# A decoder trunk on one core: layer B's softmax per token tile, attention begun with its k, and two projections moved ahead

## The chip, the cores and the metric

The kernel runs on one core of one Trainium2 chip. The metric is the time of one execution on the device in microseconds; the kernel before was timed in three runs. Beside them one execution was taken by the hardware profiler. Its page and its trace are what is read below. Engines are named PE (TensorE matmul), DVE (VectorE), ACT (ScalarE), POOL (GpSimd) and SP (SyncE, which issues the weight DMAs here).

## What is computed

A two-layer decoder trunk on 256 tokens of width 1024, all in float32. Layer A is a causal differential attention with an MLP. Then one set of keys and values is projected, and layer B attends to it: three groups of dilated windows, 16 heads of width 64, and an MLP. Cut to layer B, which the change touches:

```python
def dilated_mixer(x, norm_gain, w_q, q_gain, w_o, k_sh, v_sh, cos, sin):
    q = (rms_norm(x, norm_gain) @ w_q).reshape(B, S, G, H, D)
    q = rms_norm(q, q_gain[:, None, :])
    q = apply_rope(q.reshape(B, S, G * H, D), cos, sin).reshape(B, S, G, H, D)
    for g, (window, dilation) in enumerate(DIL_GROUPS):     # (128,1), (512,4), (2048,16)
        o_g, lse_g = dilated_group_attention(q[:, :, g], k_sh[:, :, g], v_sh[:, :, g], window, dilation)
    wts = jax.nn.softmax(jnp.stack(lses, axis=0), axis=0)   # over the three groups
    o = jnp.sum(wts[..., None] * jnp.stack(outs, axis=0), axis=0)
    return o.astype(x.dtype).reshape(B, S, H * D) @ w_o
```

Weighting the groups by their softmax denominators is the same as one softmax over the scores of all three groups, and so the kernel computes it.

## The kernel before

Every float32 product is made of three matmuls: both operands are split into a high part (ACT, a copy to the reduced type) and a low part (DVE, the difference). The weights arrive by DMA from SP in pieces of 768 KB or 1 MB (`raw`), and class `Weights` splits each half of a piece into `whi` and `wlo` (L82, L83), up to five halves ahead of their use.

Layer B works on eight pairs of heads, `hp` 0 to 7. For each pair the loop at L719 projects q (i = 0), k (i = 1) and the values (i = 2), each 384 columns for two token tiles of 128: `gemm` (L297) makes four calls of `gemm_half`, of 12 matmuls each (L292 to L294). `qk_rows` (L310) turns a tile of q or k into normalized, rotated rows: a square on ACT, the product `T` and the sums on DVE, three operations on POOL that end in `qn`. The value tiles `vt` are split on ACT and DVE (L731, L732).

The attention of a pair, `attn_B` (L596), is a Python generator. `start` puts it on a list, and `tick` (L211) lets each entry of the list go on to its next `yield`, after it has pumped the weight splits. `gemm` ticks after its first three halves and the loop at L735 once more at the end of a projection. A generator that yields n goes on n ticks later. So the numbers in `WAIT_B` say how much projection work is issued on PE between two steps of a pair's attention. The steps are:

1. `qk_T` (L352): 12 transposes of q and k rows on PE (L357), split into `th` (ACT) and `tl` (DVE).
2. Scores of tile 0 (L350) and, a step later, of tile 1. Masked passes on DVE (L369) write `sm` and the maxima.
3. The softmax: `nm` (DVE), exponentials with row sums (L618, ACT), reciprocal `rd` (DVE), scaling (L623, ACT).
4. For each of the two heads: 8 transposes of the probabilities (L632), split into `p2` (L634); then 6 matmuls with the values (L646), `ot` on ACT and DVE (L649, L650), `oT` on POOL (L651). After the second head `oT` is split into `oh` (`oTh`, ACT) and `ol` (`oTl`, DVE).

The loop over pairs before the change starts the attention of a pair after its third projection:

```python
pss = acc0 if hp == 0 and i == 0 else gemm(hx, ("B", hp, i), 384)
...
tick()
...
gens.append(start(attn_B(hp, rows[0], rows[1], vts, oh, ol)))
```

After the last projection class `OutProj` (L390) multiplies with `woB`: `body(kt)` for pairs 0 to 5, two groups of six 512-column matmuls each with a tick behind each group, and `group` (L413) for pairs 6 and 7, inside `boundary` (L372). Before these the kernel finishes the generators that are still active (L738 to L742). Pieces of weights are planned in the order of their use (L138 to L144).

The pools bound how far work can run ahead: eight PSUM banks for everything on PE, two buffers each of `sm`, `p2` and `T`, four of `th` and `tl`, three of the value tiles, six of `qn`. Within these the framework's scheduler may place an instruction on an engine earlier or later than its line in the program.

Of the kernel before, what the change touches and what calls it, by code (L numbers as in the profile page):

```python
# [10 lines left out]
F32 = mybir.dt.float32  # L11
# [5 lines left out]
P = 128  # L17
S = 256
NT = S // P
# [21 lines left out]
WAIT_B = (2, 2, 2, 2, 2, 3)  # L41

SUB = ((2, 0, 4), (3, 1, 5))

# [58 lines left out]
def trunk(ctx, tc, a):  # L103
# [17 lines left out]
    def plan(key, src, n):  # L121
        at[key] = len(chunks)
        chunks.append((src, n))
# [14 lines left out]
    for hp in range(HP):  # L138
        for i in range(3):
            for j in range(2):  # L140
                plan(("B", hp, i, j), a["wB"][hp, i, j], 4 * 384)
# [80 lines left out]
    def start(gen):  # L222
        ent = [gen, 0]
        active.append(ent)
        return ent
# [137 lines left out]
    def block(b):  # L363
        return slice(b * P, (b + 1) * P)
# [231 lines left out]
    def attn_B(hp, qr, kr, vts, oh, ol):  # L596
# [3 lines left out]
        mxs = [small.tile([P, 2], F32, name="mx", tag="mx") for _ in range(2)]  # L600
        sms = [wk.tile([P, 2, 4 * P], F32, name="sm", tag="sm") for _ in range(2)]
        for b in range(2):
            own = slice(S + b * P, S + (b + 1) * P)
            scs = [wps(), wps()]
            scores2([sc[:, 0:S] for sc in scs], T0, block(b), KALL)
            scores2([sc[:, S:S + P] for sc in scs], T1, block(b), own)
            scores2([sc[:, S + P:] for sc in scs], T2, block(b), own)
            for hh in range(2):
                masked(sms[hh][:, b, :], scs[hh], mask[:, 4 * b:4 * b + 4, :].rearrange("p b k -> p (b k)"),
                       -3e38, mxs[hh][:, b:b + 1])  # L610
            yield WAIT_B[2 + b]
        for hh in range(2):
            sm = sms[hh]
            den = small.tile([P, 2], F32, name="den", tag="den")
            nm = small.tile([P, 2], F32, name="nm", tag="nm")
            nc.vector.tensor_scalar(nm, mxs[hh], -(HD ** -0.5), None, op0=ALU.mult)
            for b in range(2):
                nc.scalar.activation(sm[:, b, :], sm[:, b, :], AF.Exp, bias=nm[:, b:b + 1], scale=HD ** -0.5,  # L618
                                     accum_out=den[:, b:b + 1])
            rd = small.tile([P, 2], F32, name="rd", tag="rd")  # L620
            nc.vector.reciprocal(rd, den)
            for b in range(2):
                nc.scalar.activation(sm[:, b, :], sm[:, b, :], AF.Copy, scale=rd[:, b:b + 1])  # L623
        yield WAIT_B[2]
# [94 lines left out]
    for hp in range(HP):  # L719
        rows = [[None] * NT, [None] * NT]  # L720
        vts = []
        for i, hx in ((0, hq), (1, hk), (2, hk)):
            pss = acc0 if hp == 0 and i == 0 else gemm(hx, ("B", hp, i), 384)
            for t in range(NT):
                ps = pss[t]
                if i < 2:
                    rows[i][t] = qk_rows(ps, 2 * G, rb[NT + t], windows(tabB[:, i, t]))
                else:
                    vt = wk.tile([P, 2 * G, 2, HD], F32R, name="v", tag="v", bufs=3)
                    psv = ps[:, :384].rearrange("p (g d) -> p g d", d=HD)  # L730
                    nc.scalar.activation(vt[:, :, 0, :], psv, AF.Copy, scale=rb[t])  # L731
                    nc.vector.scalar_tensor_tensor(vt[:, :, 1, :], psv, rb[t], vt[:, :, 0, :].bitcast(F32),  # L732
                                                   op0=ALU.mult, op1=ALU.subtract)
                    vts.append(vt)
            tick()  # L735
        gens.append(start(attn_B(hp, rows[0], rows[1], vts, oh, ol)))
# [94 lines left out]
```

## Time and profile before

| | |
|---|---|
| Median of 3 runs | 800.8 us (800.39 to 802.36) |
| Profiled execution, its own time | 801.55 us |
| Span of the profile | 799.5 us |
| Busy: PE, weight loads (PEld), DVE, ACT, POOL | 97%, 86%, 73%, 58%, 24% |
| Mean granted TensorE clock | 0.995 of full speed |
| DMA | 131.12 MB, mean 164 GB/s |

The span runs from the first to the last instruction of the profiled execution. Layer B's projections and attention lie from about 320 to 606 us, its output projection from 577 to 616 us, the second MLP behind it. A row of the timeline gives the start and the duration of one instruction or of a run of alike ones (x8), its engine, line, operation, out<-in, shapes, and in brackets how long the engine stood idle before it and who released it. PE matmuls overlap, so their starts are what counts.

### The profile page before, as it was taken

How to read it: one execution, taken by the hardware profiler on the slowest of the kernel's cores; microseconds unless marked ns; L12 is line 12 of the kernel's file. 1: busy time of each engine (PE TensorE's matmuls, PEld its weight loads, DVE VectorE, ACT ScalarE, POOL GpSimd, SP SyncE). 2: the span in 40 equal slices, each digit the busy share in tenths (PEclk: the TensorE clock that was granted, in tenths of full speed). 3: DMA queues.
4: the chain of work that ended last, by engine and by line, in shares of the span. 5: the costliest groups of instructions: out<-in, count | busy, mean ns of one | idle time of the engine just before them, and what ended most of it. 6: DMA issues, size and time to landing. Idle time of an engine off the chain costs nothing.

```text
span 799.5 us, 11766 instructions
## 1 busy us (share of the span) xinstructions
PE 772.1 (97%) x4408; PEld 686.7 (86%) x4408; DVE 581.1 (73%) x985; ACT 467.0 (58%) x851; POOL 190.9 (24%) x191
## 2 busy tenths in 40 slices
PE   6999989999999999999999999999997999999998
PEld 6898967888888888999999999999886888888886
DVE  3998987666656666998888888888767666556663
ACT  5667777544444445657586674857766544444441
POOL 2553531300000000555336354363611000000000
PEclk9999999999999999999999999999999999999999
DMA  8643445445555542554443434434442455545531
GB/s 300 229 143 123 158 155 164 169 171 197 198 176 207 171 184 90 187 198 154 136 153 113 157 121 157 158 119 172 159 158 106 158 186 182 210 170 199 187 130 52
DMA packets 22328, 131.12 MB, mean 164 GB/s; under 512 B 2560, under 2 KB 3328, under 8 KB 13056
## 3 DMA queue, kind: packets, MB, share of 16 engines
q1 hardware_dynamic: 22272, 130.38, 46.0%
q8 instruction: 34, 0.56, 0.3%
q14 instruction: 22, 0.18, 0.1%
HBM read 129.32 MB, written 1.05 MB: 163 GB/s over the span
## 4 chain that ended last, share of the span: by engine, by line
PE 64%; DVE 17%; ACT 12%; issue 3%; POOL 2%; DMA 1%; SPq 0%; POOLq 0%; DVEq 0%; ACTq 0%
PE wps L435 15%; PE wps L437 7%; PE acc L488 7%; PE acc L489 7%; PE acc L490 7%; DVE wlo L83 5%; PE acc L292 4%; PE acc L294 4%; PE acc L293 4%; ACT whi L82 4%; ACT sm L618 2%; DVE sm L369 2%; PE wps L632 2%; DVE T L317 2%; ACT smA L541 2%
## 5 line engine op out<-in xcount | busy, mean ns | idle before, releaser
L83 DVE TENSOR_TENSOR wlo<-raw,whi 128x1024 fp32r<-128x1024 f32 (+1 forms) x272 | 307.0, 1138 | 153.9 <-ACT whi L82 153.7
L82 ACT ACTIVATE whi<-raw 128x1024 fp32r<-128x1024 f32 (+1 forms) x272 | 258.9, 957 | 211.1 <-issue 74.9
L435 PE MATMUL wps<-hT,whi 128*128 128x512 f32 x512 | 182.2, 399 | 2.0 <-DVE hT L271 2.0
L437 PE MATMUL wps<-hT,wlo 128*128 128x256 f32 x512 | 142.9, 280 | 0.0
L435 PEld LDWEIGHTS wps<-hT,whi 128*128 128x128 f32 x512 | 95.9, 188 | 26.0 <-DVE hT L271 3.2
L328 POOL TENSOR_TENSOR T<-T 128x384 f32<-128x384 f32 (+1 forms) x48 | 44.4, 924 | 280.5 <-DVE ms L243 181.6
L488 PE MATMUL acc<-whi,u 128*128 128x512 f32 x256 | 100.4, 392 | 0.3 <-ACT u L340 0.3
L489 PE MATMUL acc<-wlo,u 128*128 128x512 f32 x256 | 100.0, 391 | 0.0
L490 PE MATMUL acc<-whi,u 128*128 128x512 f32 x256 | 98.9, 389 | 0.0
L437 PEld LDWEIGHTS wps<-hT,wlo 128*128 128x128 f32 x512 | 96.6, 189 | 1.4
L292 PE MATMUL acc<-whi,hT 128*128 128x384 f32 x256 | 88.8, 349 | 0.3 <-ACT whi L82 0.2
L292 PE MATMUL acc<-whi,hK 128*128 128x384 f32 x256 | 87.6, 343 | 0.0
L293 PE MATMUL acc<-wlo,hT 128*128 128x384 f32 x256 | 86.3, 337 | 1.1 <-DVE wlo L83 1.1
L294 PE MATMUL acc<-whi,hT 128*128 128x384 f32 x256 | 86.2, 337 | 0.0
L294 PE MATMUL acc<-whi,hK 128*128 128x384 f32 x256 | 85.8, 335 | 0.0
L293 PE MATMUL acc<-wlo,hK 128*128 128x384 f32 x256 | 85.7, 335 | 0.0
L332 POOL TENSOR_TENSOR f<-ms,half 128x6 f32<-128x6 f32 (+1 forms) x48 | 68.2, 1422 | 4.6 <-DVE ms L323 3.1
L488 PEld LDWEIGHTS acc<-whi,u 128*128 128x128 f32 x256 | 48.1, 188 | 11.7 <-ACT u L340 1.2
L490 PEld LDWEIGHTS acc<-whi,u 128*128 128x128 f32 x256 | 48.1, 188 | 10.6 <-DVE u L341 0.4
L489 PEld LDWEIGHTS acc<-wlo,u 128*128 128x128 f32 x256 | 48.1, 188 | 8.8
L293 PEld LDWEIGHTS acc<-wlo,hT 128*128 128x128 f32 x256 | 48.6, 190 | 1.4 <-DVE wlo L83 1.4
L292 PEld LDWEIGHTS acc<-whi,hT 128*128 128x128 f32 x256 | 48.6, 190 | 1.4 <-ACT whi L82 0.5
(117 smaller groups left out, 1204.9 us busy)
## 6 DMA issues: line engine op xcount, KB each, us to landing
raw<-in_wB SPq DMA_DIRECT2D x48, 768.0 KB, 4.2
raw<-in_wup SPq DMA_DIRECT2D x32, 1024.0 KB, 4.8
raw<-in_wdn SPq DMA_DIRECT2D x32, 1024.0 KB, 4.8
raw<-in_wA SPq DMA_DIRECT2D x15, 768.0 KB, 4.3
raw<-in_woA SPq DMA_DIRECT2D x4, 1024.0 KB, 4.8
raw<-in_woB SPq DMA_DIRECT2D x4, 1024.0 KB, 4.8
early<-in_x SPq DMA_DIRECT2D x2, 512.0 KB, 5.3
x<-in_xp SPq DMA_DIRECT2D x1, 1024.0 KB, 7.5
```

Of the source, the lines that this page charges most:

```text
L82: self.nc.scalar.activation(hi[:, :n], raw, AF.Copy)
L83: self.nc.vector.tensor_tensor(lo[:, :n], raw, hi[:, :n].bitcast(F32), op=ALU.subtract)
L292: nc.tensor.matmul(ps, h[:, kt, 0, tok], wh[:, c], start=kt == 0, stop=False)
L293: nc.tensor.matmul(ps, h[:, kt, 0, tok], wl[:, c], start=False, stop=False)
L294: nc.tensor.matmul(ps, h[:, kt, 1, tok], wh[:, c], start=False, stop=kt == KT - 1)
L328: nc.gpsimd.tensor_tensor(u[:, :n].rearrange("p (h a d) -> p h a d", a=2, d=HD // 2), T[:, 0, :n].rearrange("p (h a d) -> p h a d", a=2, d ...
L332: nc.gpsimd.tensor_tensor(f[:, :nsub], ms[:, :nsub], half[:, :nsub], op=ALU.pow)
L435: nc.tensor.matmul(o, wh[:, c], self.h[:, kt].rearrange("p l s -> p (l s)"), start=kt == 0, stop=False, skip_group_check=True)
L437: nc.tensor.matmul(o[:, 0:S], wl[:, c], self.h[:, kt, 0, :], start=False, stop=kt == KT - 1, skip_group_check=True)
L488: nc.tensor.matmul(ps, uh[:, tok], dh[:, c], start=first, stop=False)
L489: nc.tensor.matmul(ps, uh[:, tok], dl[:, c], start=False, stop=False)
L490: nc.tensor.matmul(ps, ul[:, tok], dh[:, c], start=False, stop=last)
```

## The change

Three things are done together.

- `attn_B` does the softmax of both heads for tile 0 right behind the scores of tile 0, and that of tile 1 behind the scores of tile 1. `mx`, `nm`, `den` and `rd` hold two heads of a tile where they held two tiles of a head.
- A pair's attention is started after its k projection instead of after its values; `WAIT_B` is changed with it.
- A list `PAIRS` gives the order of projections. It is the old one for pairs 0 to 5; then come q and k of pair 6, q and k of pair 7, the values of pair 6, the values of pair 7. The weight pieces are planned in that order.

```diff
-WAIT_B = (2, 2, 2, 2, 2, 3)
+WAIT_B = (4, 2, 2, 3, 2, 3)
...
+PAIRS = [(hp, i) for hp in range(HP - 2) for i in range(3)]
+PAIRS += [(HP - 2 + e, i) for e, i in ((0, 0), (0, 1), (1, 0), (1, 1), (0, 2), (1, 2))]
...
-    for hp in range(HP):
-        for i in range(3):
-            for j in range(2):
-                plan(("B", hp, i, j), a["wB"][hp, i, j], 4 * 384)
+    for hp, i in PAIRS:
+        for j in range(2):
+            plan(("B", hp, i, j), a["wB"][hp, i, j], 4 * 384)
...
-        mxs = [small.tile([P, 2], F32, name="mx", tag="mx") for _ in range(2)]
         sms = [wk.tile([P, 2, 4 * P], F32, name="sm", tag="sm") for _ in range(2)]
         for b in range(2):
...
+            mx = small.tile([P, 2], F32, name="mx", tag="mx")
             for hh in range(2):
                 masked(sms[hh][:, b, :], scs[hh], mask[:, 4 * b:4 * b + 4, :].rearrange("p b k -> p (b k)"),
-                       -3e38, mxs[hh][:, b:b + 1])
-            yield WAIT_B[2 + b]
-        for hh in range(2):
-            sm = sms[hh]
+                       -3e38, mx[:, hh:hh + 1])
+            nm = small.tile([P, 2], F32, name="nm", tag="nm")
+            nc.vector.tensor_scalar(nm, mx, -(HD ** -0.5), None, op0=ALU.mult)
             den = small.tile([P, 2], F32, name="den", tag="den")
-            nm = small.tile([P, 2], F32, name="nm", tag="nm")
-            nc.vector.tensor_scalar(nm, mxs[hh], -(HD ** -0.5), None, op0=ALU.mult)
-            for b in range(2):
-                nc.scalar.activation(sm[:, b, :], sm[:, b, :], AF.Exp, bias=nm[:, b:b + 1], scale=HD ** -0.5,
-                                     accum_out=den[:, b:b + 1])
+            for hh in range(2):
+                nc.scalar.activation(sms[hh][:, b, :], sms[hh][:, b, :], AF.Exp, bias=nm[:, hh:hh + 1],
+                                     scale=HD ** -0.5, accum_out=den[:, hh:hh + 1])
             rd = small.tile([P, 2], F32, name="rd", tag="rd")
             nc.vector.reciprocal(rd, den)
-            for b in range(2):
-                nc.scalar.activation(sm[:, b, :], sm[:, b, :], AF.Copy, scale=rd[:, b:b + 1])
-        yield WAIT_B[2]
+            for hh in range(2):
+                nc.scalar.activation(sms[hh][:, b, :], sms[hh][:, b, :], AF.Copy, scale=rd[:, hh:hh + 1])
+            yield WAIT_B[2 + b]
...
-    for hp in range(HP):
-        rows = [[None] * NT, [None] * NT]
-        vts = []
-        for i, hx in ((0, hq), (1, hk), (2, hk)):
-            pss = acc0 if hp == 0 and i == 0 else gemm(hx, ("B", hp, i), 384)
...
-            tick()
-        gens.append(start(attn_B(hp, rows[0], rows[1], vts, oh, ol)))
+    rows, vts = {}, [[] for _ in range(HP)]
+    for hp, i in PAIRS:
+        hx = hk if i else hq
+        pss = acc0 if hp == 0 and i == 0 else gemm(hx, ("B", hp, i), 384)
...
+        tick()
+        if i == 1:
+            gens.append(start(attn_B(hp, *[[rows[hp, e, t] for t in range(NT)] for e in range(2)], vts[hp],
+                                     oh, ol)))
```

## Rows read from the trace of the kernel before

**Rows 1.** Busy time by stretch, pair 3: length, PE, PEld, DVE, ACT, POOL, clock, DMA.

```profile
439.20:473.00 33.80, 33.24 (x223) 31.68 (x222) 27.82 (x48) 22.67 (x41) 15.78 (x16) 1.00 0.42 141
```

**Rows 2.** Timeline of PE, pair 0: start us, us, engine, line, operation.

```profile
370.26 0.33 PE L294 MATMUL acc<-whi,hK 128*128 128x384 f32 x1
...
370.78 0.34 PE L294 MATMUL acc<-whi,hK 128*128 128x384 f32 x1
...
371.75 0.42 PE L292 MATMUL acc<-whi,hK 128*128 128x384 f32 x1
```

**Rows 3.** Waits of PE, 345 to 575 and 575 to 622: total us, times, longest.

```profile
PE wps L632 <- ACT sm L623: 3.9, 6, 1.0
...
PE wps L646 <- DVE p L341: 0.9, 1, 0.9
```

**Rows 4.** Timeline of PE around the transposes of pair 2's probabilities.

```profile
437.28 0.34 PE L294 MATMUL acc<-whi,hK 128*128 128x384 f32 x1
438.20 1.27 PE L632 MATMUL wps<-ident,sm 128*128 128x128 f32 x8 [0.58 <-ACT sm L623]
439.23 0.42 PE L292 MATMUL acc<-whi,hK 128*128 128x384 f32 x1
```

**Rows 5.** Timeline of PE at the end of the output projection's bodies.

```profile
605.58 0.40 PE L404 MATMUL acc<-whi,oTl 128*128 128x512 f32 x1
606.92 1.22 PE L646 MATMUL wps<-p,v 128*128 128x512 f32 x6 [0.94 <-DVE p L341]
610.78 0.53 PE L402 MATMUL acc<-whi,oTh 128*128 128x512 f32 x1 [2.65 <-ACT oTh L340]
...
614.53 1.04 PE L260 MATMUL wps<-ident,x 128*128 128x128 f32 x8
```

**Rows 6.** Timeline of PE, pair 3, from pair 2's last PV on.

```profile
452.96 1.10 PE L646 MATMUL wps<-p,v 128*128 128x512 f32 x6
453.89 0.33 PE L292 MATMUL acc<-whi,hK 128*128 128x384 f32 x1
...
456.10 0.39 PE L350 MATMUL wps<-th,tl 64*128 64x256 f32 x2
...
462.84 0.44 PE L292 MATMUL acc<-whi,hK 128*128 128x384 f32 x1
...
471.99 1.27 PE L632 MATMUL wps<-ident,sm 128*128 128x128 f32 x8 [0.56 <-ACT sm L623]
```

**Rows 7.** Busy time by stretch, behind the long wait of the tail.

```profile
610.70:614.50 3.80, 3.72 (x9) 2.80 (x10) 1.81 (x3) 1.04 (x4) 0.00 (x0) 0.55 0.51 216
```

**Rows 8.** Timeline of ACT, the scaling passes of pair 2.

```profile
437.44 2.54 ACT L623 ACTIVATE sm<-sm,rd 128x512 f32<-128x512 f32 x4
```

**Rows 9.** Timeline of DVE and ACT, the softmax of pair 7.

```profile
593.47 0.68 DVE L369 CUSTOM_DVE_ANT_0 sm<-wps,mask 128x512 f32<-128x512 f32 x1
...
595.61 0.71 ACT L618 ACTIVATE sm<-sm,nm 128x512 f32<-128x512 f32 x1
...
597.02 1.32 ACT L623 ACTIVATE sm<-sm,rd 128x512 f32<-128x512 f32 x2
...
598.96 1.04 ACT L82 ACTIVATE whi<-raw 128x1024 fp32r<-128x1024 f32 x1
```

**Rows 10.** Timeline of DVE, rows of q, and the end of pair 2's attention.

```profile
453.31 0.94 DVE L317 TENSOR_TENSOR T<-acc,tabB 128x768 f32<-128x768 f32 x1
...
457.18 0.68 DVE L650 TENSOR_TENSOR ot<-wps,ot 64x512 f32<-64x512 f32 x1
...
460.97 0.42 DVE L341 TENSOR_TENSOR oTl<-oT,oTh 128x256 fp32r<-128x256 f32 x1 [1.98 <-ACT oTh L340]
```

**Rows 11.** Waits of all engines, 340 to 620: total us, times, longest.

```profile
ACT oTh L340 <- POOL oT L651: 24.7, 8, 3.5
```

**Rows 12.** Timeline of POOL and PE in pair 0's k rows and pair 1's q.

```profile
346.00 0.83 POOL L334 TENSOR_TENSOR qn<-T,f 128x384 f32<-128x384 f32 x1
...
346.03 0.33 PE L292 MATMUL acc<-whi,hT 128*128 128x384 f32 x1
```

More of the change, by code (lines that the diff above doesn't have):

```diff
@@ L718, in trunk @@
     gens = []
-    for hp in range(HP):
-        rows = [[None] * NT, [None] * NT]
-        vts = []
-        for i, hx in ((0, hq), (1, hk), (2, hk)):
-            pss = acc0 if hp == 0 and i == 0 else gemm(hx, ("B", hp, i), 384)
[L724 to L734, printed above, removed]
-            tick()
-        gens.append(start(attn_B(hp, rows[0], rows[1], vts, oh, ol)))
+    rows, vts = {}, [[] for _ in range(HP)]
+    for hp, i in PAIRS:
+        hx = hk if i else hq
+        pss = acc0 if hp == 0 and i == 0 else gemm(hx, ("B", hp, i), 384)
+        for t in range(NT):
+            ps = pss[t]
+            if i < 2:
+                rows[hp, i, t] = qk_rows(ps, 2 * G, rb[NT + t], windows(tabB[:, i, t]))
+            else:
+                vt = wk.tile([P, 2 * G, 2, HD], F32R, name="v", tag="v", bufs=3)
+                psv = ps[:, :384].rearrange("p (g d) -> p g d", d=HD)
+                nc.scalar.activation(vt[:, :, 0, :], psv, AF.Copy, scale=rb[t])
+                nc.vector.scalar_tensor_tensor(vt[:, :, 1, :], psv, rb[t], vt[:, :, 0, :].bitcast(F32),
+                                               op0=ALU.mult, op1=ALU.subtract)
+                vts[hp].append(vt)
+        tick()
+        if i == 1:
+            gens.append(start(attn_B(hp, *[[rows[hp, e, t] for t in range(NT)] for e in range(2)], vts[hp],
+                                     oh, ol)))
     op = OutProj("oB", oh, ol)
```

## The prediction

> **What bounds the kernel now.** I read first how busy the engines are over one pair of layer B [rows 1]: of 33.8 us TensorE (PE) works 33.24, VectorE (DVE) 27.82, ScalarE (ACT) 22.67. That names PE, but the ends of matmuls are modelled, so I counted from start to start. Three 384-column matmuls of a projection take 0.52 us (370.26 to 370.78 [rows 2]), and this spacing fills the stretch between the attention pieces. Work on ACT, DVE and POOL is free there unless PE waits for it, so the next view was PE's waits. From 345 to 575 us there is one kind: the transposes of the probabilities (L632) wait six times for the last pass of the softmax on ACT (L623). In the tail PE waits once for the split of `p` [rows 3] and once for `oTh` [rows 5]. All that the change can win is in these eight places; after 622 us nothing is touched.
>
> What they cost, by starts. Pair 0 shows L632 unhindered: the last matmul before it starts at 370.78, the first behind it at 371.75, so 0.97 us [rows 2]. At pair 2 it is 437.28 to 439.23, 1.95 us, a loss of 0.98; the listed wait of 0.58 misses the part inside the group [rows 4]. Five of the six are like it; the sixth is the longest, 1.0 listed [rows 3], so 0.98 + 0.42 = 1.4. Together 5 x 0.97 + 1.4 = **6.2 us**. The tail: the nine matmuls from 610.78 take 3.75 us [rows 5] at a granted clock of 0.55, nearly all at the 1.2 GHz level, right behind PE's long wait [rows 7]; at full clock they would take 3.75 x 0.55 = 2.06, 0.23 each, so 1.7 us are lost there. The matmul of 605.58 should have been followed 0.23 later, at 605.81, and 606.92 came: 1.1 us. Six PV matmuls (L646) take 0.93 us elsewhere (452.96 to 453.89 [rows 6]), so after those of 606.92 the next was due at 607.85, and 610.78 came: 2.9 us. Together **5.7 us**.
>
> **The change part by part.** The unit is a half: 12 matmuls of a projection, 4 x 0.52 = 2.08 us. I follow the generator through its ticks (three inside a projection, one at its end; after a wait of n it goes on n ticks later).
>
> *No arithmetic is added or removed.* Per pair there are still four masked passes, four exponentials, four scaling passes, two `nm` and two `rd` of the same shapes, and the same splits. The 48 weight DMAs on SP keep size and count; only the pieces of pair 7's q and k go ahead of those of pair 6's values, as their uses do. So busy time stays, and queue positions move.
>
> *Softmax per token tile.* Before: scores of tile 0, two halves, scores of tile 1, two halves, then all the softmax is issued, two halves, L632. ACT runs four exponentials and then four scaling passes; the first of these (2.54 us for four from 437.44) ends at about 438.1, and L632 starts at 438.20 [rows 4, 8]. So the data is late. After: tile 0 is finished while projections still run, and from tile 1's scores to L632 there are three halves, and four transposes of tile 0 go first: 6.24 + 0.4 = 6.6 us. What must fit is best seen in the tail of before, where the queues are nearly empty: tile 1's masked passes start at 593.47, two exponentials of 0.71 end at 596.32, then the reciprocal and one scaling pass (1.32 / 2 = 0.66): about 597.3, with the hand-over from PE some 4.0 us [rows 9]. That leaves 2.6 us for queueing. Ahead of tile 1's masks stand, on DVE, the row work of the next pair's q (two T of 0.94, two sums and two small ones, 3.5 us), issued over 3 us before these scores end: a remainder of at most 1 us with a weight split [rows 10]; ACT may put a weight pass of 1.04 at most between [rows 9]. About 2 us, under 2.6. Bounds for the wait that remains: 0 (back to back there is nothing more to gain) and 2.5 us, if the path is as long as now (462.84 to 471.99, 9.1 us [rows 6]). I take 0.1 us a pair, near zero, because those 9.1 us hold two exponentials and a delayed issue that move away: 0.7 us over seven pairs.
>
> *Attention begun with its k.* The transposes of q and k (L357) move two halves earlier, to the first half of the next projection, right behind the last PV of the pair before. The `ot` pass, the second value tile and `oTl` of that pair now share this place with the three `tl`, on DVE. Today `tl` is done when T starts at 453.31, and the scores start at 456.10, 2.8 us later [rows 6, 10]. Ahead of them come at most 0.68 (`ot`) + 0.68 (the value tile, which is narrower than `ot`) + 0.42 (`oTl`) = 1.8 us, so nothing is paid. What is moved past POOL helps: today `oT` queues behind the row work of the new q, and ACT stands 24.7 us in all for it, DVE behind it [rows 10, 11]. With the last PV one half into the projection POOL has no rows queued. I cost this gain at nothing, as PE does not see it, but it makes the 0.1 above likely. L357 needs the rows of k, three operations on POOL for each token tile. **Pair 0 pays**: its last k rows leave POOL at 346.83 (346.00 + 0.83), and L357 now comes when the second half of pair 1's q starts, at 346.03 [rows 12]. Three transposes run first (0.3 us), so about 0.6 us; between 0 and 0.9. From pair 1 on POOL starts with no backlog, and the distance from k's end is a whole projection, one half and the L632 and L646 groups between, about 14 us: nothing.
>
> *q and k of pair 7 ahead of the values of pair 6.* Now all of pair 7's scores, softmax and PV lie in the output projection. After, its L357 and tile 0's scores lie in the last projection; then six matmuls of the output projection (6 x 0.23 = 1.36 us) are a step, twelve in all: scores of tile 1 after step 1, L632 after step 4, first PV after 6, last PV after 9. Softmax: 3 x 1.36 + 0.1 + 0.4 = 4.6 us against 4.0. First PV: two steps from its L632, as now, where it does not wait (the one wait of L646 for `p` is the last PV's [rows 3, 5]). Last PV: three steps instead of one. `oTh`: 3.86 us from the last PV to its user (606.92 to 610.78 [rows 5]); now the PV, three steps and three matmuls, 0.9 + 4.1 + 0.7 = 5.7. So both tail waits go, and the slow clock with them. A weight pass of 1.04 on ACT can fall into the softmax [rows 9]: 0 to 1.6 us, I take 0.6, as only part of it shows beyond the spare 0.6. Banks: two accumulators of the last projection, four of the output, one PV and two scores make nine of eight for a moment; the split of a value tile, two passes of at most 0.68, frees one, within that bound. Four row projections (6 and 7) follow each other, where now a value projection comes after two; POOL's operations of one fit into one, so I cost it at nothing, and the room is the 14 us above.
>
> **Sum**, against the profiled execution's own 801.55 us (span 799.5 and 2.05 around it): - 6.2 - 5.7 + 0.7 + 0.6 + 0.6 = - 10.0, so 791.5. The median of the runs is 800.8, 0.75 lower; I forecast **790.8 us**.
>
> **The rivals.**
> *The pairs win nothing.* If 1 us more of queue than I count stands before the last scaling pass, L632 waits as before. For it: DVE is busy 27.82 of 33.8 us [rows 1]. Against: the 2.6 us and POOL's knot undone. Time: 800.8 - 5.7 + 0.6 + 0.6 = 796.3. A second way to it is that the gap is a buffer's; the scaling pass that ends right before the transposes [rows 4, 8] speaks against that. (The Trainium skill, Perfetto Trace Analysis, under Identifying Performance Opportunities, says that the same gap repeated on the engine that should be saturated can mean too little SBUF or PSUM for the next tile. By that rule the change, which adds no buffer, would leave the six gaps and come out at this rival's time.)
> *The tail waits again*, for a bank or for pair 7's softmax: 800.8 - 6.2 + 0.7 + 0.6 = 795.9.
> *Slower.* Tile 1's masks stay queued behind the q rows, so that the path from scores to scaling keeps its 9.1 us while its room falls to 6.6: 2.5 us for each of seven pairs. 7 x 2.5 - 6.2 - 5.7 + 0.6 + 0.6 = + 6.8, so 807.6. It makes the kernel slower from 1.5 us a pair on (10.7 / 7).
> *It does not do what it says*: the order on ACT and DVE is the planner's, and it may put tile 0's exponentials beside tile 1's and pair 7's work late: 800.8.
>
> **How the numbers follow.** Forecast 0.63 (its own range 788.5, with all costs nil, to 793.5, with the remaining waits at 0.5 us a pair), pairs win nothing 0.12, tail waits 0.09, slower 0.11, no effect 0.05. Range 788.4 to 797.0: the forecast and the two half-gains, 0.84. About 0.3%, 2.4 us, is what a measurement of this kernel can tell from no change: faster 0.84, within 0.05, slower 0.11.
>
> **What would show it.** Right: no PE wait of L632 for L623 from 372 to 575; pair periods of 32.8 us instead of 33.8; L357 straight behind L646; no PE gap over 1 us from the last projection to the boundary, and a granted clock of 1.0 there; one short wait of L357 for `qn` near 346. Wrong: L632 waiting again, or L350 for `tl`, or L646 for `p`, in every pair; the forecast falls if these come to over 0.5 us a pair.

## The result, and the profile after

The changed kernel takes **810.1 us** (median of 4, 809.2 to 811.4) against 801.4 for the kernel before on the same chip: ratio 1.0110 [1.0090, 1.0131], 1.1% slower. The forecast was 790.8, faster. The profiled execution took 809.95 us with a span of 808.2, so the spans are 8.7 us apart, and that is what has to be found.

Line numbers of after: L632 and L646 are the same two operations as before; the scores are L353, the transposes of q and k L360, the projections L295 to L297, the weight splits L86 (upper half, ACT) and L87 (lower half, DVE), the split helper L343 (ACT) and L344 (DVE), the masks L372.

PE's waits from 345 to 575 us, and then from 575 to 625 (total us, times, longest), beside [rows 3]:

```profile
PE wps L632 <- ACT sm L623: 5.6, 6, 1.0
PE wps L646 <- DVE p L344: 5.4, 6, 0.9
PE wps L353 <- DVE tl L344: 2.0, 1, 2.0
...
PE wps L632 <- ACT sm L623: 2.6, 1, 2.6
```

The wait that the change was to remove is still there in all six pairs, and a second one of the same size has joined it in all six: the PV matmuls wait for the lower half of the split of `p`. The two tail waits of before, for `p` and for `oTh`, are gone; two others stand in their place.

One pair, as in [rows 1]: length, then PE, PEld, DVE, ACT, POOL, clock, DMA share, GB/s.

```profile
434.79:469.86 35.07, 33.23 (x222) 31.74 (x220) 28.54 (x48) 22.80 (x42) 17.61 (x14) 1.00 0.39 136
```

PE's work is what it was (33.23 against 33.24), and the pair is 1.27 us longer. By starts, PE in this pair's successor:

```profile
463.51 0.44 PE L295 MATMUL acc<-whi,hK 128*128 128x384 f32 x1
...
469.86 0.60 PE L632 MATMUL wps<-ident,sm 128*128 128x128 f32 x4
471.39 0.66 PE L632 MATMUL wps<-ident,sm 128*128 128x128 f32 x4 [0.94 <-ACT sm L623]
471.80 0.42 PE L295 MATMUL acc<-whi,hK 128*128 128x384 f32 x1
...
477.12 1.21 PE L646 MATMUL wps<-p,v 128*128 128x512 f32 x6 [0.90 <-DVE p L344]
478.17 1.03 PE L632 MATMUL wps<-ident,sm 128*128 128x128 f32 x8
```

Tile 1's scores end where 463.51 begins. The first four transposes, those of tile 0, are ready; the second four come 1.53 behind them. The whole group takes 1.94 (469.86 to 471.80), elsewhere in this trace 0.79, so 1.15 are lost. From 471.80 to the next transposes at 478.17 lie 24 matmuls of the projection and six of PV, 6.37 us; the same thirty in pair 0 of before, where nothing waits, take 5.18 (from 371.75 [rows 2] to 376.93), so 1.19 are lost. The six pairs are 0 to 5, and the two waits are alike in all of them: 6 x (1.15 + 1.19) = **14.0 us**, where the prediction counted 6.2 for before.

Why both are late is in one stretch of DVE and ACT. DVE, behind the same scores:

```profile
464.06 2.96 DVE L87 TENSOR_TENSOR wlo<-raw,whi 128x768 fp32r<-128x768 f32 x2 [0.28 <-ACT whi L86]
466.93 0.68 DVE L372 CUSTOM_DVE_ANT_0 sm<-wps,mask 128x512 f32<-128x512 f32 x1
...
468.27 0.17 DVE L615 TENSOR_SCALAR nm<-mx 128x2 f32<-128x2 f32 x1
...
472.72 0.96 DVE L87 TENSOR_TENSOR wlo<-raw,whi 128x768 fp32r<-128x768 f32 x1 [1.00 <-ACT whi L86]
473.60 0.95 DVE L320 TENSOR_TENSOR T<-acc,tabB 128x768 f32<-128x768 f32 x1
...
474.92 0.95 DVE L320 TENSOR_TENSOR T<-acc,tabB 128x768 f32<-128x768 f32 x1
475.79 1.28 DVE L344 TENSOR_TENSOR p<-wps,p 128x512 fp32r<-128x512 f32 x2
```

and ACT:

```profile
468.47 0.72 ACT L618 ACTIVATE sm<-sm,nm 128x512 f32<-128x512 f32 x1 [3.71 <-DVE nm L615]
...
469.90 0.83 ACT L86 ACTIVATE whi<-raw 128x768 fp32r<-128x768 f32 x1
470.63 1.32 ACT L623 ACTIVATE sm<-sm,rd 128x512 f32<-128x512 f32 x2
471.86 0.83 ACT L86 ACTIVATE whi<-raw 128x768 fp32r<-128x768 f32 x1
472.59 0.84 ACT L318 ACTIVATE sq<-acc 128x384 f32<-128x384 f32 x2
473.33 0.84 ACT L86 ACTIVATE whi<-raw 128x768 fp32r<-128x768 f32 x1
474.07 1.06 ACT L343 ACTIVATE p<-wps 128x512 fp32r<-128x512 f32 x2
```

The scores are there at about 463.5, and DVE begins two weight splits of the next projection. The masks of tile 1 start at 466.93, 3.4 us after their data. ACT stands in its queue with an exponential that needs `nm`, and is idle for 3.71 us. All that stands behind that exponential on ACT (a weight split, the squares, another weight split) is then done between the scaling and the split of `p`, so that `p` starts at 474.07 instead of about 472. By this order both waits of PE go back to the same two splits; in the second the row work of k (473.60 to 475.79) also stands on DVE ahead of the lower half of `p`. Over the kernel ACT is idle for `nm` for 29.8 us, in the trace of before for 14.2.

Towards the end the waits are of the same kind. In pair 6 the scores wait for the third `tl`, which stands on DVE behind an `oTl` of the pair before:

```profile
563.65 0.43 DVE L344 TENSOR_TENSOR oTl<-oT,oTh 128x256 fp32r<-128x256 f32 x1 [2.54 <-ACT oTh L343]
563.99 0.68 DVE L344 TENSOR_TENSOR tl<-wps,th 128x512 fp32r<-128x512 f32 x1
...
600.16 0.43 DVE L344 TENSOR_TENSOR oTl<-oT,oTh 128x256 fp32r<-128x256 f32 x1 [0.64 <-ACT oTh L343]
600.50 0.68 DVE L372 CUSTOM_DVE_ANT_0 sm<-wps,mask 128x512 f32<-128x512 f32 x1
```

The `oT` that this chain waits for ran on POOL at 562.44, straight behind the row operations of q of pair 7 (554.61 to 562.36). PE loses 2.2 us there (18 score matmuls take 3.40, elsewhere 1.18) and 1.5 in the 24 matmuls behind (5.93 against 4.39). In pair 7 the second mask of tile 1 starts at 600.50, 4.4 us behind its scores (596.06): a weight split, a value tile, an `ot` and, between the two masks, an `oTl` of the pair before stand ahead of it on DVE, and 1.1 us of waiting for ACT. From pair 7's first transpose of the probabilities (600.25) to 604.72 PE takes 4.47 us for eight transposes and two matmuls, elsewhere 0.79 + 0.46: 3.2 lost, and 1.1 more in the ten matmuls behind (3.39 against 2.27). Behind both waits the granted clock falls to a mean between the 1.2 and the 2.4 GHz level, as in [rows 7]:

```profile
565.30:571.23 5.93, 5.93 (x26) 5.68 (x25) 5.61 (x13) 3.85 (x9) 2.29 (x2) 0.71 0.47 177
...
604.72:608.11 3.39, 3.39 (x13) 2.75 (x11) 2.45 (x3) 1.93 (x3) 0.00 (x0) 0.68 0.56 237
```

Sum of after: 14.0 + 2.2 + 1.5 + 3.2 + 1.1 + 0.6 at the front = 22.6 us lost, against 6.2 + 5.7 = 11.9 that the prediction counted for before: 10.7, where the spans differ by 8.7. Of the 2.0 between them some 1.2 are losses of before which that count left out: 0.7 from 610.78 to 616.68 [rows 5] (5.90 us for twelve matmuls of 0.23 and 0.79 of transposes, with 1.7 counted), and 0.09 in each of six pairs (33.80 us [rows 1] against 32.74 in a run below that hardly waits, with 0.97 counted). Another 0.6 is that layer B begins earlier in the trace of after: the second group of transposes of `x` ahead of it starts at 321.20, before the change at 321.84. The last 0.2 was not traced.

### The profile page after: what moved, and what is told of

Read it like the earlier page. It is cut to its first block, busy times and chain, and to the rows that moved or that the text cites. A ratio compares the mean times of both kernels' runs of the same rounds, so it can differ in the third digit from the quotient of the medians.

```text
span 808.2 us, 11734 instructions
## 1 busy us (share of the span) xinstructions
PE 772.6 (96%) x4408; PEld 688.6 (85%) x4408; DVE 587.4 (73%) x985; ACT 467.4 (58%) x851; POOL 201.0 (25%) x191
## 3 DMA queue, kind: packets, MB, share of 16 engines
HBM read 129.32 MB, written 1.05 MB: 161 GB/s over the span
## 4 chain that ended last, share of the span: by engine, by line
PE 62%; DVE 17%; ACT 13%; POOL 4%; issue 3%; DMA 1%; SPq 0%; DVEq 0%; POOLq 0%; ACTq 0%
PE wps L438 14%; PE acc L491 7%; PE wps L440 7%; PE acc L492 7%; PE acc L493 7%; DVE wlo L87 6%; PE acc L295 4%; PE acc L297 4%; PE acc L296 4%; ACT whi L86 3%; ACT sm L618 2%; DVE sm L372 2%; ACT sm L623 2%; DVE T L320 2%; POOL f L335 2%
## 5 line engine op out<-in xcount | busy, mean ns | idle before, releaser
L87 DVE TENSOR_TENSOR wlo<-raw,whi 128x1024 fp32r<-128x1024 f32 (+1 forms) x272 | 309.5, 1146 | 157.8 <-ACT whi L86 157.6
L86 ACT ACTIVATE whi<-raw 128x1024 fp32r<-128x1024 f32 (+1 forms) x272 | 258.1, 957 | 216.6 <-issue 72.6
L331 POOL TENSOR_TENSOR T<-T 128x384 f32<-128x384 f32 (+1 forms) x48 | 49.3, 1027 | 281.6 <-DVE ms L246 181.6
L295 PE MATMUL acc<-whi,hT 128*128 128x384 f32 x256 | 89.0, 350 | 0.3 <-ACT whi L86 0.2
L295 PE MATMUL acc<-whi,hK 128*128 128x384 f32 x256 | 88.3, 346 | 0.0
L297 PE MATMUL acc<-whi,hK 128*128 128x384 f32 x256 | 86.3, 337 | 0.0
L297 PE MATMUL acc<-whi,hT 128*128 128x384 f32 x256 | 86.1, 337 | 0.0
L337 POOL TENSOR_TENSOR qn<-T,f 128x384 f32<-128x384 f32 (+1 forms) x48 | 52.8, 1099 | 3.8
L295 PEld LDWEIGHTS acc<-whi,hT 128*128 128x128 f32 x256 | 48.4, 189 | 1.9 <-ACT whi L86 0.5
```

The source lines that it names most:

```text
L86: self.nc.scalar.activation(hi[:, :n], raw, AF.Copy)
L87: self.nc.vector.tensor_tensor(lo[:, :n], raw, hi[:, :n].bitcast(F32), op=ALU.subtract)
L295: nc.tensor.matmul(ps, h[:, kt, 0, tok], wh[:, c], start=kt == 0, stop=False)
L297: nc.tensor.matmul(ps, h[:, kt, 1, tok], wh[:, c], start=False, stop=kt == KT - 1)
L337: nc.gpsimd.tensor_tensor(qn[:, :n].rearrange("p (h d) -> p h d", d=HD), u[:, :n].rearrange("p (h d) -> p h d", d=HD), f[:, :nsub, None].t ...
```

## Experiments

Two theories stood against each other. **Place**: DVE, ACT and POOL have the time, but in their queues, which run in order, weight splits that nobody needs yet stand ahead of masks and of `p`, for which PE waits. **Load**: a softmax in two parts with a shorter room asks more of DVE and ACT than they can do in that time, wherever the splits stand. In between stood the question which of the three parts of the change does the harm. The kernel before was timed beside every run (medians 801.4 to 801.8); "gain" and "loss" are against it.

### The parts one by one

**The softmax per token tile alone** (begun behind the values, as before, all pairs in plain order, and with the PE steps where the kernel before has them):

```
-WAIT_B = (2, 2, 2, 2, 2, 3)
+WAIT_B = (2, 2, 2, 4, 2, 3)
...
+            nc.vector.tensor_scalar(nm, mx, -(HD ** -0.5), None, op0=ALU.mult)
...
+            for hh in range(2):
+                nc.scalar.activation(sms[hh][:, b, :], sms[hh][:, b, :], AF.Copy, scale=rd[:, hh:hh + 1])
+            yield WAIT_B[2 + b]
```

> The first part alone: softmax per token tile, but the attention starts behind the values, the projections keep their plain order, and the waits (2, 2, 2, 4, 2, 3) put every step on PE where it was before. Theory (the loss is where the steps now lie: masks of tile 1 behind row work and weight splits, the split of p behind the row work of k): here four halves, 8.7 us, lie between tile 1's scores and L632 and the path took 7.7 us in the changed kernel, and L632 falls away from the row work, so neither L632 nor L646 waits between 345 and 575 us; the six waits of before (6.2 us) go, 794 to 797 us. Rival (the per-tile softmax itself is slower, because ACT stands at the head of its queue for nm twice a pair, 29.8 us in all where it was 14.2): L632 still waits about 1 us a pair, 800 us or more.

Measured: 828.0 us, ratio 1.0326 [1.0308, 1.0345]. The theory that this part alone is a gain fell at once. As its rival had it, L632 still waits about 1 us a pair, but the larger wait is one that neither had. PE's waits from 345 to 575 us, and two rows of DVE:

```profile
PE wps L646 <- DVE p L344: 13.1, 6, 2.4
PE wps L632 <- ACT sm L623: 5.5, 5, 1.1
```

```profile
483.85 4.39 DVE L87 TENSOR_TENSOR wlo<-raw,whi 128x768 fp32r<-128x768 f32 x4
488.16 1.28 DVE L344 TENSOR_TENSOR p<-wps,p 128x512 fp32r<-128x512 f32 x2
```

Four weight splits in a row, 4.39 us on DVE (and 3.04 on ACT), stand ahead of the split of `p`. In the kernel before, where all exponentials are issued together and late, such splits stand apart on ACT: one between the exponentials, one ahead of the scaling, one ahead of `p` (433.85, 436.71 and 439.89 in pair 2).

**The begin with k alone** (the kernel before with its old softmax):

```
-WAIT_B = (2, 2, 2, 2, 2, 3)
+WAIT_B = (4, 2, 2, 2, 2, 3)
...
-        gens.append(start(attn_B(hp, rows[0], rows[1], vts, oh, ol)))
+            if i == 1:
+                gens.append(start(attn_B(hp, rows[0], rows[1], vts, oh, ol)))
```

> The second part alone: attention begun with its k (first wait 4), the old softmax over the whole pair, plain order of the projections. L632 comes one half behind the rows of k. Theory (place): its softmax is queued around the row work of k, so L632 keeps a wait of 1 us or more in each pair; the split of p, one half behind the rows, is on time; 800 to 806 us, of which the later end of pair 7's attention costs up to 4. Rival (the softmax per tile makes the loss, the start does not): 797 to 801 us.

Measured: 803.4 us, ratio 1.0018 [1.0009, 1.0027]. The time is in the theory's range, but the waits came out the other way round: the six of L632 are gone without any change of the softmax, and five of L646 for `p` (4.0 us together) and four at the end (2.0, 1.7, 1.5, 0.8 us) came instead. In sum 1.6 us are lost. Which order in the queues of DVE and ACT does this was not traced.

**The changed kernel without the moved projections**:

```
-PAIRS += [(HP - 2 + e, i) for e, i in ((0, 0), (0, 1), (1, 0), (1, 1), (0, 2), (1, 2))]
+PAIRS += [(HP - 2 + e, i) for e in range(2) for i in range(3)]
```

> The changed kernel without its third part: pairs 6 and 7 are projected in the plain order. Theory: every pair pays the two waits as in the changed kernel (about 1.15 + 0.97 us at L632 and L646), now pair 6 too, and pair 7's attention ends late, with PE standing for oTh before the last groups and the clock falling, as before: 812 to 817 us. Rival (the loss sits in the moved projections, where L350 waits 2.0 and L632 2.6 us): 800 to 806 us.

Measured: 809.4 us, ratio 1.0099 [1.0084, 1.0114], as the changed kernel, and less than the 812 to 817 expected. Its steady waits are the same to the digit (5.6 and 5.4 us). So in the changed kernel moving the projections takes away at the end about what it brings there.

**The changed kernel with the old softmax**, the other two parts kept:

```
-WAIT_B = (4, 2, 2, 3, 2, 3)
+WAIT_B = (4, 2, 2, 2, 2, 3)
...
+            yield WAIT_B[2 + b]
+        for hh in range(2):
...
+            nc.vector.tensor_scalar(nm, mxs[hh], -(HD ** -0.5), None, op0=ALU.mult)
```

> The changed kernel without its first part: attention begun with its k and the moved projections, but the softmax over the whole pair as before (waits 4, 2, 2, 2, 2, 3). Theory (the softmax per tile makes the loss: exponentials come early in ACT's queue, ACT stands for nm, the weight copies behind it pile up in front of the split of p): without it the pairs lose about what the second part alone showed (five waits of L646, 4.0 us in all, none of L632), and the moved projections take away part of the tail's waits (2.0, 1.7, 1.5 and 0.8 us there): 796 to 801 us. Rival (the moved projections are what costs, as POOL's rows of four projections follow each other): 804 us or more.

Measured: 799.4 us, ratio 0.9975 [0.9965, 0.9985]: 2 us better than before, and 10.7 better than the change. The softmax per token tile, from which 6.2 us of gain were expected, is what costs. Beside the begin with k alone, the moved projections are worth 3.7 us here (2.1 gained instead of 1.6 lost), of the 5.7 forecast.

### More room

The changed kernel with four halves instead of three between tile 1's scores and L632:

```
-WAIT_B = (4, 2, 2, 3, 2, 3)
+WAIT_B = (4, 2, 2, 4, 2, 3)
```

> The changed kernel with four halves instead of three between tile 1's scores and L632 (waits 4, 2, 2, 4, 2, 3). Theory: 6.6 us of room become 8.7, against a path of 7.7, and L632 lies a half behind the rows of k, so L632's wait of 1.15 us a pair goes and most of L646's 0.97 with it: 12 us less than the changed kernel, 795 to 800 us. Rival (DVE is short of time over the whole pair, so that whatever lies behind waits): the period of a pair stays near 35 us, 806 us or more.

Measured: 814.5 us, ratio 1.0156 [1.0141, 1.0171]. PE's waits from 345 to 575 us:

```profile
PE wps L646 <- DVE p L344: 13.3, 6, 2.5
```

Half of the theory held: from 345 to 575 us the wait of L632 is gone. The other half fell, and the time and the pair period (35.2 us) are those of the rival: DVE still runs 2.95 us of two weight splits ahead of tile 1's masks, ACT still stands 3.71 us for `nm`, and the work that piles up behind is now put ahead of `p`, where the wait grows from 0.9 to 2.5. More room did not help here, as the queue held the wrong thing first; it moved the wait to the next step. After this run, as before it, place and load were both still possible.

### Without the weight splits

To see whether the splits are at all what the softmax waits for, layer B's splits were left out from pair 1 on (the pieces of pair 0 are used again; DMAs kept), once in each of the three kernels:

```
+        if c in self.same:
+            self.parts[c, i] = self.parts[self.first, (self.half // 2) % 2]
+            self.half += 1
+            self.fetch()
+            return True
...
+    W.first = at["B", 0, 2, 1]
+    W.same = range(at["B", 1, 0, 0], at["oB", 0])
```

> The kernel before, with the splitting of layer B's weights left out from pair 1 on: its projections use the last split pieces of pair 0 again (so the output is another), the DMAs run as ever. It takes about 0.85 us of ACT and 0.95 us of DVE per half out of the queues and is the measure for the next two runs. Both theories: the six waits of L632 shrink or go, 794 to 798 us.

> The softmax per token tile alone (as in the first experiment, 828 us), with the splitting of layer B's weights left out from pair 1 on in the same way. Theory (the loss is the weight splits that pile up ahead of the split of p): with them gone the 2.4 us waits of L646 go in pairs 1 to 6, the time comes within 4 us of the same cut of the kernel before. Rival (the softmax per tile is itself too slow, through the turns that ACT and DVE take for nm, exponentials and rd): L632 and L646 keep waits of over 1 us a pair, at least 10 us more than that cut.

> The changed kernel with the splitting of layer B's weights left out from pair 1 on in the same way. Theory: the waits of L632 (1.15 us) and L646 (0.97 us) go from pair 1 on and the time falls below the same cut of the kernel before, as the prediction had it, by 2 to 8 us. Rival (place beside the row work of k is enough to make p late without any weight split): L646 keeps about 1 us a pair, and the time lies above that cut.

Measured: kernel before without the splits 799.5 us (797.1 to 804.6), 0.9979 [0.9961, 0.9996]; the softmax part alone 796.4, 0.9937 [0.9919, 0.9955]; the change 792.4, 0.9888 [0.9865, 0.9910]. The kernel before, the fastest of the three with the splits, is the slowest without them, and the change comes out 1.6 us above the forecast, with less work. PE's waits in it from 345 to 575 (PV is L654 here, the scores L361):

```profile
PE wps L654 <- DVE p L352: 0.6, 1, 0.6
PE wps L361 <- DVE tl L352: 0.5, 1, 0.5
```

and its pair period is 32.74 us (L632 at 463.19 and at 495.93), where 32.8 were forecast. So the splits are the cause. It doesn't tell place from load, since both vanish with them. The kernel before gained little because one wait of 6.2 us for the scaling passes came up in it in pair 2, and its tail waits stayed; why that single wait comes was not pursued.

### All the work, in another order

Now the splits stay, and only their place changes. The changed kernel, with the splits of the next projection held back from tile 0's `nm` until tile 1's masks have been issued, and their lower halves put behind tile 1's `nm` on DVE:

```
     def tick():
-        W.pump()
         for ent in list(active):
...
+        if not W.hold:
+            W.pump()
...
+        with self.tc.issue_after(self.behind) if self.behind is not None else nullcontext():
+            self.nc.vector.tensor_tensor(lo[:, :n], raw, hi[:, :n].bitcast(F32), op=ALU.subtract)
...
+            W.behind = nc.vector.tensor_scalar(nm, mx, -(HD ** -0.5), None, op0=ALU.mult).ins
+            W.hold = b == 0
```

> The changed kernel with all of its work, and one thing of its order changed: where tile 1's scores have just been issued, the weight splits of the next projection wait until tile 1's masked passes and nm have been issued, and the lower halves of these splits stand behind nm on DVE. ACT's order is as in the changed kernel. Theory (the place of the weight splits in the queue, not their sum, makes the softmax late): the masks of tile 1 start some 3 us earlier (two passes of 1.48 no longer ahead of them), the path of 7.8 us falls to about 5, under the room of 6.6, and the six waits of L632 for L623 (1.15 us a pair by starts) go. L646 waits for the lower half of p on DVE, which the delayed splits can push either way: it keeps its 0.97 us a pair (then 810.1 - 6.9 = 803) or loses it too (797). Rival (load: DVE and ACT have no time for the splits inside a shorter softmax, wherever they stand): what L632 gains L646 loses, the sum of both waits stays near 2.1 us a pair, 808 to 812.

Measured: **795.8 us**, ratio 0.9935 [0.9911, 0.9958], 14.3 us below the changed kernel (794.1 to 799.4; the trace is of the slowest). The pump also stands behind the generators at every tick now; up to 345 us PE's waits are those of the changed kernel to 0.1 us, so that this changes nothing in layer A. From 345 to 575 us neither the transposes of the probabilities nor PV is among PE's waits any more. One pair, then DVE and ACT behind tile 1's scores, which end at 457.76 (masks are L376 here, splits L87 and L89, exponentials L623, scaling L628, the split of `p` L347 and L348):

```profile
457.76:490.80 33.04, 33.03 (x222) 31.79 (x220) 28.76 (x49) 22.97 (x42) 16.91 (x15) 1.00 0.41 144
```

```profile
457.87 0.69 DVE L376 CUSTOM_DVE_ANT_0 sm<-wps,mask 128x512 f32<-128x512 f32 x1
...
459.22 0.34 DVE L619 TENSOR_SCALAR nm<-mx 128x2 f32<-128x2 f32 x1
459.47 1.82 DVE L89 TENSOR_TENSOR wlo<-raw,whi 128x768 fp32r<-128x768 f32 x2
...
461.29 4.18 DVE L89 TENSOR_TENSOR wlo<-raw,whi 128x768 fp32r<-128x768 f32 x4
...
466.26 1.27 DVE L348 TENSOR_TENSOR p<-wps,p 128x512 fp32r<-128x512 f32 x2
```

```profile
459.60 0.72 ACT L623 ACTIVATE sm<-sm,nm 128x512 f32<-128x512 f32 x1 [1.05 <-DVE nm L619]
...
461.76 1.32 ACT L628 ACTIVATE sm<-sm,rd 128x512 f32<-128x512 f32 x2
...
465.06 1.09 ACT L347 ACTIVATE p<-wps 128x512 fp32r<-128x512 f32 x2
```

DVE does as much as in the changed kernel (28.76 us a pair against 28.54), and six lower halves lie between the masks and `p`, where the changed kernel has two: the two that stood ahead of tile 1's masks are among them, and two that stood ahead of tile 0's. PE waits at neither step; weight loads wait 0.3 us a pair for a lower half, and the pair takes 33.04 us where 32.74 were reached without splits. From the scores' end to the scaling pass it is 4.0 us (457.76 to 461.76), where it was 7.1 (463.51 to 470.63); ACT's idle time for `nm` is 1.05 instead of 3.71, and with that `p` is early too: it starts on ACT 0.64 behind L632's start (464.42), in the changed kernel 4.2 behind (469.86 to 474.07). Load is refuted for these two waits, place is shown. One thing was expected wrong: ACT's order is not quite that of the changed kernel, as one weight split also came to stand behind `p` there. How much of L646's gain is due to that alone, or to the two further lower halves, was not separated.

The same test from the other side: the softmax part alone (the 828.0 us), with three of the four splits that stood ahead of `p` put behind its first pass on both engines, and the pump held back at the tick ahead of L632:

```
+        with self.tc.issue_after(self.behind[0]) if self.behind is not None else nullcontext():
+            self.nc.scalar.activation(hi[:, :n], raw, AF.Copy)
...
+                    behind = split(p2[:, b, :, 0], p2[:, b, :, 1], pp.rearrange("p (i q) -> p i q", i=4))
+            if hh == 0:
+                W.behind = behind
```

> The kernel with the softmax per token tile alone (828.0 us), with all of its work; changed is only that of the four weight splits that ACT and DVE ran ahead of the split of p (3.04 us on ACT, 4.39 us on DVE), three stand behind the first pass of the split of p. Theory (place): L646's wait for p, 2.4 us in each of six pairs, falls by 2 us or more, so 828 - 12 = 816 or less, and the delayed weights are needed later than p, so that nothing else waits over 0.5 us a pair. Rival (load: the two engines have no spare time there, and what is put behind p makes the next projection's weights late): the wait moves to the projection's matmuls, for the splits, and the time stays above 824.

Measured: 804.9 us, ratio 1.0042 [1.0027, 1.0057]; 23 us less than with the splits in front, for the same work. PE's only wait from 345 to 575 is the one that was not touched (L643 is the transposes of the probabilities here), and DVE ahead of tile 1's masks, whose scores end at 463.41:

```profile
PE wps L643 <- ACT sm L629: 6.2, 5, 1.4
```

```profile
466.01 0.17 DVE L627 RECIPROCAL rd<-den 128x2 f32<-128x2 f32 x1 [1.59 <-ACT sm L624]
...
468.70 0.96 DVE L90 TENSOR_TENSOR wlo<-raw,whi 128x768 fp32r<-128x768 f32 x1 [1.00 <-ACT whi L88]
469.58 0.68 DVE L378 CUSTOM_DVE_ANT_0 sm<-wps,mask 128x512 f32<-128x512 f32 x1
```

By this trace load does not make this wait either: of the 6.2 us from the scores to the masks DVE stands idle for 3.2 (1.59, 0.57 and 1.00), for tile 0's exponentials and for upper halves on ACT, while its next masks are ready. It is of the kind that the rival of the first run named: the two engines wait for each other in turn.

The 12 us expected for the place were too few. The 13.1 us of L646 went, and at the end two of three waits for `p`.

### The end, and a version that beats both

The masks first, and in each tick the newest attention served ahead of the older one, so that `tl` of a pair is issued ahead of the last PV, `ot` and `oTl` of the pair before:

```
-        for ent in list(active):
+        for ent in reversed(list(active)):
```

> As the kernel with the masks first, and in each tick the newest attention is served ahead of the older one, so that the transposes of q and k of a pair are issued ahead of the last PV of the pair before. It aims at the end alone: the wait of 2.0 us of pair 6's scores for tl, which stands behind oTl on DVE, and the 2.6 us of pair 7's transposes of the probabilities. Theory (a queue order again): L353's wait for tl goes, 2 us less than the kernel with the masks first; in the steady pairs nothing changes by more than 0.3 us a pair. Rival (POOL's four row projections in a row are themselves too late, not oTl's place): the 2.0 us stay and the time is that of the kernel with the masks first.

Measured: 796.7 us, 0.9936 [0.9924, 0.9949], the time of the run without it. The wait for `tl` in layer B is gone, as the theory had it; but the loop also serves layer A, where PE now waited 5.6 us for `mx` and `nm` and 2.1 for a value tile, and no longer 4.1 for `tl`. So the rival's time came out for another reason than the rival's, and the last run keeps the newest first to layer B:

```
+        for ent in (reversed(list(active)) if W.newest else list(active)):
...
+    gens, W.newest = [], True
```

> The kernel with the masks first and the newest attention first, the second now in layer B only (in layer A it brought PE waits of L364 for mx and nm and of L409 for v, about 3 us up to 260 us of the trace, that the kernel with the masks first alone does not have). Theory: the gains of the two add: no steady wait of L637 or L651, no wait of L357 for tl, layer A as in the kernel before; the profiled span is 3 us below the 793.5 of the run with newest first everywhere, 790 to 791, the median 792 to 794. Rival (what layer A lost was given back elsewhere): 796 to 797 again.

Measured: **792.9 us** (791.7 to 794.4), ratio 0.9898 [0.9882, 0.9915]; the profiled span is 789.8. PE's waits in it from 345 to 575 us, and the one from 575 to 640 (L300 is a projection, L364 the transposes of q and k, L637 those of the probabilities):

```profile
PE acc L300 <- DVE wlo L89: 0.4, 1, 0.4
PE wps L364 <- POOL qn L341: 0.4, 1, 0.4
...
PE wps L637 <- ACT sm L628: 1.1, 1, 1.1
```

From 345 to 640 us 1.9 us of listed waits are left, of 7.8 before and 16.1 in the changed kernel, and the granted clock is 1.00 in every stretch from 345 to 616. All three parts of the change are in this kernel.

## Why the prediction was wrong

By its own steps:

- **What bounds the kernel** was right: PE's work per pair stayed (33.23 us), its waits decided, and every kernel here is told apart by them.
- **"A remainder of at most 1 us with a weight split"** on DVE ahead of tile 1's masks is the step that failed. The row work of q was over 0.3 us behind the scores (463.78), as allowed. But two weight splits stood behind it, and it was 3.4 us from the scores to the masks. The rest of the path was sized right: masks and `nm` 1.54 (466.93 to 468.47), exponentials 1.43, a weight split on ACT 0.73 (1.04 allowed), the first scaling pass 0.66: 4.4, of which the softmax is 3.6, against 4.0 forecast with the hand-over. The path is 7.9 us (463.51 to 471.39), for a room of 6.6. The weight splits were in the argument only as one remainder [rows 10] and one pass of 1.04 on ACT [rows 9]. The 4.0 and the 1.04 came from the tail, where the queues are nearly empty. That the loop issues up to two splits at every step stands in the code and wasn't followed, and the trace of before has two in this very place, with tile 1's masks 2.3 us behind their scores (462.84):

```profile
463.40 1.82 DVE L83 TENSOR_TENSOR wlo<-raw,whi 128x768 fp32r<-128x768 f32 x2
465.14 0.68 DVE L369 CUSTOM_DVE_ANT_0 sm<-wps,mask 128x512 f32<-128x512 f32 x1
```

- **The split of `p`** was given no term in the sum; it appeared only under "Wrong". It costs 1.19 a pair, 7.1 us, more than the whole expected steady gain. From L632 to L646 there are two halves before and after, and so it was taken over from before. But what stands ahead of `p` in the queues is not taken over: in the kernel before ACT waits 1.83 us for `nm` in such a pair and then runs without a pause to its last scaling pass, the splits in between; here what it could not do in 3.71 us of waiting is put in front of `p`.
- **Attention begun with k**, "nothing is paid": right in pairs 1 to 5; in pair 6 it is 2.2 us, and 1.5 of slow clock. The front was right: 0.6 expected, 0.59 measured (12 transposes in 1.82 instead of 1.23).
- **"POOL has no rows queued"** is true in the steady pairs and false where the four row projections follow each other. That is the point at which the prediction says "I cost it at nothing": it cost 3.7 us, for `oT` stood behind the rows of q of pair 7, `oTh` behind `oT`, `oTl` behind `oTh`, and `tl` behind `oTl`, through three queues.
- **The tail**: both old waits and the slow clock from 610.7 on are gone, as forecast. The softmax of pair 7 was given 0.6 us late; it is 3.2, and slow clock behind it 1.1. The two new waits cost more than the two old ones (8.0 against 5.7).

In sum, against the 11.9 lost before: steady + 0.7 for L632 (6 x 1.15 against 6.2) and + 7.1 for L646; the end + 2.3, the front + 0.6. A slip in the prediction carries nothing: its "788.5, with all costs nil" is 788.9 by its own terms (800.8 - 6.2 - 5.7).

**Of the rivals** "slower" gave 807.6, for 810.1 measured, and its place is the right one: tile 1's masks late on DVE, over 1.5 us a pair. What stood ahead of them was not the rows of q, which it named, but weight splits; and of its 2.5 us at L632 only 1.15 came there, the other 1.19 at L646, where nothing was forecast. The place and the sign were right, half of the mechanism was not. That the time came near is in part luck: this rival gave the pairs 17.5 us, where they lost 14.0, and let the end gain 5.7, where it lost 2.3. "The pairs win nothing" put L632's place right, and no more. The rule of the Trainium skill that was weighed there (Perfetto Trace Analysis, Identifying Performance Opportunities: a gap that repeats on the engine that should be saturated can mean too little SBUF or PSUM) does not hold for this gap: the kernel with the masks first has the same buffers, and the gap is closed in all six pairs.

The mechanism itself, that two half softmaxes let PE go on, was sound: with the splits out of the way by their place alone the pair takes 33.04 us, and the end put right as well gives 792.9, 2.1 above the forecast, with an order of the queues that the changed kernel does not have.

## What to carry to other kernels

When a piece of work is cut in two and given less room, don't add up what its own operations take: list, for each engine, everything that the code issues between its inputs and its consumer, the background work of the loop included, and take the order of the queues from there. Here two engines that hand work to each other made the wait double: while ACT stood 3.7 us for DVE's `nm`, its own queue grew, and the next consumer, which had nothing to do with the first, was late by what had piled up. Before giving more room to a step that is late, look whether something not yet needed stands ahead of it; putting the splits behind `nm` was worth 14.3 us here, one more half of room cost 4.4.

## What was not expected of the hardware

The lower weight split of 128x768 takes 0.95 to 0.96 us in most places (472.72 above) and 1.48 in the pair at 464.06, which began 0.40 before an operation of POOL. POOL in the changed kernel, the same operation twice:

```profile
461.13 1.02 POOL L331 TENSOR_TENSOR T<-T 128x384 f32<-128x384 f32 x1 [6.69 <-DVE T L320]
...
464.46 1.73 POOL L331 TENSOR_TENSOR T<-T 128x384 f32<-128x384 f32 x1
```

It takes 1.73 there, 0.71 more than alone, and the two splits together 2.96, 1.14 more than two elsewhere (1.82 at 564.59). One order fits all numbers: the first split to about 465.0, then POOL's operation to about 466.1, then the second split to 467.0. By the Trainium skill (SBUF — State Buffer, SBUF: two separate sides) a DVE operation with two inputs in SBUF and a POOL operation that reads SBUF exclude each other for a whole instruction and don't share the bandwidth. These rows agree; no run here took POOL's operation away. Of the 3.4 us by which tile 1's masks are late, about one is then POOL's, and it was in no step of the prediction.
